# A sample turn's scores and values in six TensorE runs instead of twelve

## The chip, the core and the metric

The kernel runs on one core of a Trainium2 chip. The core has five engines that each work through their own list of instructions: PE (matrix products; PEld is its loading of weights), DVE (vectors), ACT (functions such as exp), POOL (a second vector engine) and SP, which here issues nearly all DMAs, one after the other. The metric is the device time of one execution in microseconds (us). A profile is one execution with a hardware trace. Names such as `out<-in,in` are the program's tiles, and L1290 is line 1290 of the kernel.

## What is computed

One step of a small decoder: a recurrent layer, then an attention layer with a forget gate. There are two inputs. The prompt is one new sequence of 2048 tokens. The sample is 8 sequences of 8 new tokens each, and each of them attends to 4096 earlier keys and values, which lie in a cache of pages of 128 rows and are found through a page table. The part that the change touches is the sample's attention, 16 heads of 64 numbers, all in 32-bit floats:

```python
s = jnp.einsum('bqhd,bkhd->bhqk', q, k).astype(jnp.float32) * (HEAD_DIM ** -0.5)
s = s + jnp.swapaxes(cq, 1, 2)[:, :, :, None] - jnp.swapaxes(ck, 1, 2)[:, :, None, :]
s = jnp.where(mask[None, None], s, -jnp.inf)
p = jax.nn.softmax(s, axis=-1)
return jnp.einsum('bhqk,bkhd->bqhd', p.astype(v.dtype), v)
```

## The kernel before, in words

The prompt's work fills PE from the first microsecond to the last: projections with every product split in three (tiles `kv`, `qg`, lines L387 to L389), then the prompt's attention (scores `st` in L1651 and L1652, row maxima `sx` in L1438, products with the values `ops` in L1675), then the output projection (`y`). The sample's attention is laid beside it.

**A turn** is one of the 8 sample sequences with one half of the heads; there are 16 turns. A turn reads 32 pages of keys and 32 of values, four pages to a tile of 1 MB (`raw`, L1144 and L1146, four DMAs on SP). So it has eight key tiles k0 to k7 and eight value tiles v0 to v7. A key tile is turned by two DVE transposes into `ktr` (L1218). After four key tiles (a group) the two halves pp = 0 and 1 of the heads can each be scored: 32 small matmuls `dS<-ktr,qw` of 32 by 128 (L1202; the trace shows 64 of them, two for each). They write one bank of PSUM, and DVE subtracts that from the tile `sc` (L1207) and takes a maximum (L1208) before the next scores may use the bank. `softmax` then does the maxima (`dm`), the exponentials on ACT, the sums (`dsum`) and transposes `sc` on DVE. A value tile is multiplied by eight small matmuls `dO<-raw,sc` of 32 by 256 (L1290; 16 in the trace), and the last one, v7, takes the new tokens' own rows in as well (`dO<-rawn,dpc`, L1295). The result goes out through `ob` and `dres`. Small matmuls of `dS` and `dO` use a quarter of the array's columns each, four such column groups side by side.

**A run** is a row of such small matmuls on PE with nothing between them: `together` (L124) issues the first matmul of a list, and binds the rest right behind it. With `beside=True` the first one may not come ahead of the prompt's latest score matmul (`place["T"]`, `behind`, L115). With `after` the first one waits for the DMAs that are given. Two runs can also happen to fall next to each other.

**The order.** The first two turns run beside the projections with `ahead=False`, each turn by itself. The other 14 run with `ahead=True`: `period` mixes the values of turn t with the keys of turn t+1, in the order v5 (of the turn before), k0, v6, k1, v7, k2, k3, v0, k4, v1, k5, v2, k6, v3, k7, v4. The tiles share four buffers (`nraw` = 4), so a tile is asked for when the tile that had its buffer has been transposed (keys) or multiplied (values). `Later` puts a run off by one or two ticks, and `Side` paces all of it beside the prompt's work by estimated costs. A scheduler then sets the final order on each engine from those instructions, their priorities and their dependencies.

Of the kernel before, what the change touches and what calls it, by code (L numbers as in the profile page):

```python
# [90 lines left out]
def tile_hawk_fox(  # L91
# [18 lines left out]
    def tt(eng, out, a, b, op):  # L110
        eng.tensor_tensor(out, a, b, op=op)  # L111
# [990 lines left out]
    def decode(es, turns, nraw, nktr, ahead):  # L1102
# [24 lines left out]
        def bank(name, tag="d"):  # L1127
            return psum["dec"].tile([P, 512], F32, name=name, tag=tag, bufs=1)
# [42 lines left out]
        class Turn:  # L1171


            def __init__(self, it):
                self.b, self.hg, self.odd = *turns[it], it % 2
                self.next = turns[it + 1] if it + 1 < len(turns) else None
                self.dl, self.raws = Later(), []

        def begin(t):
            t.gmx = pool.tile([P, 3, 8], F32, name="gmx", tag="gmx")  # L1180
            G.memset(t.gmx[:, 2, :], NEG)

        def keys(t, xs):
# [12 lines left out]
            def scores(g, pp, kt):  # L1196

                sp = bank("dS", "d" if ahead or pp == 0 else "o")

                def score(h, x, c):  # L1200
                    i0 = (h * 2 + x) * 32 + c * 8
                    return T.matmul(sp[c * 32:(c + 1) * 32, h * P:(h + 1) * P], qw[:, pp * 2 + h // 2, h % 2 * 2 + x, :],  # L1202
                                    kt[:, :, :, i0:i0 + 8], start=(x == 0), stop=(x == 1))

                together([partial(score, h, x, c) for h in range(4) for x in range(2) for c in range(4)], beside=True)
                sv = t.sc[:, g * 4:(g + 1) * 4, :, pp * 4:(pp + 1) * 4, :].rearrange("p n a h i -> p h (n a) i")
                tt(V, sv, sp[:, :].rearrange("p (h n i) -> p h n i", h=4, n=16), sv, ALU.subtract)  # L1207
                V.tensor_reduce(gmx[:, g, pp * 4:(pp + 1) * 4], sv, axis=AX.XY, op=ALU.max)  # L1208

            for x in xs:  # L1210
                g, n = divmod(x, 4)
                if n == 0:
                    t.kts = [pool.tile([P, 4, 4, 256], F32, name="ktr", tag="ktr", bufs=nktr) for _ in range(2)]
                raw, _ = pages(cache_k, b, hg, x)
                if x == (3 if ahead else 0):
                    fetch_c()
                for pp in range(2):
                    behind("V", V.transpose(t.kts[pp][:, n], raw[:, :, pp * 256:(pp + 1) * 256]).ins)  # L1218
# [58 lines left out]

        def values(t, xs):

            dl = t.dl  # L1280
            b, hg, pc = t.b, t.hg, t.pc
            if xs[0] == 0:
                t.op = bank("dO", "o")
            op = t.op

            def products(i, raw, came, rown=None):

                def mm(m, a):
                    c = ((i + m) % 2 * 2 + a) * 32
                    return T.matmul(op[c:c + 32, :256], t.sc[:, i // 4, m, a * 4:(a + 1) * 4, :].rearrange("p h q -> p (h q)"),  # L1290
                                    raw[:, m, a * 256:(a + 1) * 256],
                                    start=(i + m < 2), stop=(i + m == NPG - 1))
# [5 lines left out]
                mms = [partial(mm, m, a) for m in range(4) for a in range(2)]  # L1298
                if rown is not None:
                    mms += [partial(new, a) for a in range(2)]  # L1300
                together(mms, came, True)

            for x in xs:
                raw, came = t.raws.pop(0) if t.raws else pages(cache_v, b, hg, x)
                if x == 5:
                    t.rown = new_rows(b, hg)
# [3 lines left out]
                dl.tick()  # L1310
                yield 2 * PV
            if xs[-1] < 7:
                return
            dl.flush()
# [13 lines left out]
        def period(p, t, n):  # L1328


            chain_ = softmax(t)
            if n:
                begin(n)
            for who, x in (("v", 5), ("k", 0), ("v", 6), ("k", 1), ("v", 7), ("k", 2), ("k", 3), ("v", 0), ("k", 4),
                           ("v", 1), ("k", 5), ("v", 2), ("k", 6), ("v", 3), ("k", 7), ("v", 4)):
                if (who, x) == ("v", 0):
                    yield from chain_
                if who == "k" and n:
                    yield from keys(n, [x])
                elif who == "v" and (t if x < 5 else p):  # L1340
                    yield from values(t if x < 5 else p, [x])
                if x > 4 or who == "k" and x < 4:
                    yield from islice(chain_, 2)
# [6 lines left out]
        yield from keys(ts[0], range(8))  # L1350
        if ahead:
            for p, t, n in zip([None] + ts, ts, ts[1:] + [None]):
                yield from period(p, t, n)
            yield from values(ts[-1], [5, 6, 7])
        else:
            for t, n in zip(ts, ts[1:] + [None]):
# [658 lines left out]
```

## Time and profile before

| | us |
|---|---|
| median of 3 timed runs | 2931.59 |
| lowest, highest | 2919.55, 2937.87 |
| the profiled execution's own time | 2919.81 |
| its span in the trace | 2918.1 |
| its mean granted TensorE clock | 0.978 |

The profile's page gives the busy time of each engine and the span in 40 slices of 73 us. A timeline lists one engine's instructions in order of time: start, length, engine, line, operation, tiles, shape and count of equal ones that follow each other, and in brackets the idle time before it with what ended it. Matmuls overlap, so the room that one takes is read from start to start, not from its length. The list of waits says which instruction stood idle for which, how long in all, how often, and the longest.

### The profile page before, as it was taken

The page shows a single profiled execution, that of the slowest core. Times are in us where ns is not written, and L with a number is a line of the kernel's source. Part 1 is how long each engine was busy: PE and PEld are TensorE (multiplying, and loading weights), DVE is VectorE, ACT ScalarE, POOL GpSimd, SP SyncE. Part 2 cuts the span into 40 slices and gives each one's busy share as a digit, 9 for nine tenths or more (in the row PEclk, how much of TensorE's full clock was granted, in tenths as well). Part 3 has the DMA queues.
Part 4 walks back from the last instruction along what each step waited for, and adds up shares of the span by engine and source line. Part 5 has one row for each costly group of instructions (what it writes and reads, how often), then busy time and mean ns, then how long its engine had stood idle before and what let it go on. Part 6 is the DMA issues. An engine that isn't in the chain of part 4 may idle for free.

```text
span 2918.1 us, 59421 instructions
## 1 busy us (share of the span) xinstructions
PE 2747.1 (94%) x21086; PEld 2224.8 (76%) x21086; DVE 1828.1 (63%) x3971; ACT 1267.6 (43%) x2874; POOL 1098.0 (38%) x1207
## 2 busy tenths in 40 slices
PE   5998999999998999999999999999999999999998
PEld 5997789988898997887888766565666665666787
DVE  7877457244256775676565676767677766655465
ACT  4656342222234665533334345444444544455221
POOL 1654110000003652100001265756565655659554
PEclk9999999999999999999999999999999999999999
DMA  4224536789745536689999978778788777862454
GB/s 127 80 86 125 169 124 188 203 243 300 224 142 177 178 107 191 215 303 325 341 314 333 338 261 293 239 255 277 253 271 269 255 259 240 284 222 61 131 184 131
DMA packets 484789, 636.03 MB, mean 218 GB/s; under 512 B 100888, under 2 KB 293145, under 8 KB 477276
## 3 DMA queue, kind: packets, MB, share of 16 engines
q1 hardware_dynamic: 484204, 630.13, 66.6%
q8 instruction: 167, 2.74, 0.4%
q0 software_dynamic: 288, 2.10, 0.3%
q14 instruction: 130, 1.06, 0.1%
HBM read 512.78 MB, written 133.85 MB: 222 GB/s over the span
## 4 chain that ended last, share of the span: by engine, by line
PE 55%; DMA 9%; DVE 7%; ACT 4%; SPq 3%; issue 2%; POOL 1%; DVEq 0%; ACTq 0%; POOLq 0%
PE ops L1675 8%; PE st L1651 5%; PE sx L1438 4%; PE st L1652 4%; PE dS L1202 3%; PE dO L1290 3%; PE y L389 3%; PE y L387 3%; PE y L388 3%; DMA raw<-in_cache_k_dram 2%; PE kv L387 2%; PE kv L389 2%; PE kv L388 2%; PE qg L387 2%; PE qg L389 2%
## 5 line engine op out<-in xcount | busy, mean ns | idle before, releaser
L1218 DVE STREAM_TRANSPOSE ktr<-raw 128x1024 f32<-128x1024 f32 x256 | 308.0, 1225 | 97.6 <-DMA raw<-in_cache_k_dram 73.5
L1440 DVE TENSOR_REDUCE mxs<-sx 128x1 f32<-128x512 f32 x384 | 253.8, 680 | 157.6 <-PE sx L1438 156.8
L387 PE MATMUL kv<-wh,xh 128*128 128x256 f32 (+3 forms) x1088 | 307.7, 287 | 3.0 <-ACT wh L432 1.7
L389 PE MATMUL kv<-wh,xl 128*128 128x256 f32 (+3 forms) x1088 | 307.1, 284 | 0.4 <-DMA xl<-xld 0.4
L388 PE MATMUL kv<-wl,xh 128*128 128x256 f32 (+3 forms) x1088 | 306.6, 284 | 0.4 <-DVE wl L433 0.3
L433 DVE SCALAR_TENSOR_TENSOR wl<-wst,gv,wh 128x256 fp32r<-128x256 f32 (+1 forms) x384 | 171.1, 494 | 130.7 <-ACT wh L432 130.6
L432 ACT ACTIVATE wh<-wst,gv 128x256 fp32r<-128x256 f32 (+1 forms) x384 | 164.4, 499 | 200.4 <-DMA wst<-in_b_w_in_dram 83.0
L389 PE MATMUL qg<-xh,wl 128*128 128x384 f32 (+2 forms) x640 | 227.5, 357 | 2.2 <-DVE wl L433 2.2
L387 PE MATMUL qg<-xh,wh 128*128 128x512 f32 (+2 forms) x640 | 229.2, 359 | 0.0
L388 PE MATMUL qg<-xl,wh 128*128 128x512 f32 (+2 forms) x640 | 228.1, 358 | 0.0
L387 PEld LDWEIGHTS kv<-wh,xh 128*128 128x128 f32 (+1 forms) x1088 | 201.1, 186 | 8.7 <-issue 3.7
L389 PEld LDWEIGHTS kv<-wh,xl 128*128 128x128 f32 (+1 forms) x1088 | 202.3, 186 | 3.1 <-issue 2.4
L388 PEld LDWEIGHTS kv<-wl,xh 128*128 128x128 f32 (+1 forms) x1088 | 201.5, 186 | 4.1 <-issue 2.5
L1166 POOL TENSOR_TENSOR qw<-qb,amask 128x128 f32<-128x128 f32 x64 | 26.7, 422 | 459.9 <-PE dS L1202 197.7
L1662 ACT ACTIVATE attl<-st 128x512 f32<-128x512 f32 (+3 forms) x236 | 120.5, 524 | 129.2 <-PE st L1652 61.4
L1444 DVE CUSTOM_DVE_ANT_0 sx<-sx,maskb 128x128 f32<-128x128 f32 (+3 forms) x256 | 123.1, 488 | 70.9 <-PE sx L1438 64.9
L1662 ACT ACTIVATE attw<-st 128x512 f32<-128x512 f32 (+3 forms) x224 | 118.0, 550 | 102.4 <-PE st L1652 68.1
L1290 PE MATMUL dO<-raw,sc 128*32 128x256 f32 x2048 | 141.9, 398 | 20.7 <-DMA raw<-in_cache_v_dram 19.9
L111 POOL TENSOR_TENSOR atth<-atth,attl 128x512 f32<-128x512 f32 (+3 forms) x119 | 128.1, 1079 | 65.9 <-ACT attl L1662 47.7
L111 POOL TENSOR_TENSOR atth<-atth,attw 128x512 f32<-128x512 f32 (+3 forms) x116 | 132.3, 1141 | 38.9 <-ACT attw L1662 22.1
L1202 PE MATMUL dS<-ktr,qw 128*32 128x128 f32 x4096 | 129.8, 282 | 14.4 <-DVE ktr L1218 13.5
L925 ACT COPY kf<-kv 128x256 f32<-128x256 f32 (+1 forms) x136 | 49.0, 366 | 217.1 <-PE kv L389 152.7
(359 smaller groups left out, 7651.8 us busy)
## 6 DMA issues: line engine op xcount, KB each, us to landing
raw<-in_cache_k_dram SPq DMA_DIRECT2D x512, 256.0 KB
raw<-in_cache_v_dram SPq DMA_DIRECT2D x512, 256.0 KB
wst<-in_w_kv_dram SPq DMA_DIRECT2D x48, 512.0 KB
wst<-in_b_w_in_dram SPq DMA_DIRECT2D x48, 512.0 KB
xt<-in_x_prompt_dram SPq DMA_DIRECT2D x32, 512.0 KB
wst<-in_a_w_in_dram SPq DMA_DIRECT2D x64, 256.0 KB
out_dram<-kf SPq DMA_DIRECT2D x128, 128.0 KB
cb<-cd SPq DMA_DIRECT2D x14, 1024.0 KB
```

The source lines that it names most:

```text
L111: eng.tensor_tensor(out, a, b, op=op)
L387: T.matmul(ps, lh(k), rh(k), start=(k == 0), stop=False)
L388: T.matmul(ps, lh(k), rl(k), start=False, stop=False)
L389: end = T.matmul(ps, ll(k), rh(k), start=False, stop=(k == nk - 1))
L432: A.activation(wh[:, k, :], st[:, k, :], AF.Copy, scale=gk)
L433: V.scalar_tensor_tensor(wl[:, k, :], st[:, k, :], gk, f(wh[:, k, :]), op0=ALU.mult, op1=ALU.subtract)
L1202: return T.matmul(sp[c * 32:(c + 1) * 32, h * P:(h + 1) * P], qw[:, pp * 2 + h // 2, h % 2 * 2 + x, :], kt[:, :, :, i0:i0 + 8], start=(x = ...
L1218: behind("V", V.transpose(t.kts[pp][:, n], raw[:, :, pp * 256:(pp + 1) * 256]).ins)
L1290: return T.matmul(op[c:c + 32, :256], t.sc[:, i // 4, m, a * 4:(a + 1) * 4, :].rearrange("p h q -> p (h q)"), raw[:, m, a * 256:(a + 1) * ...
L1440: r = V.reduce_max(mx[:, j, ck:ck + 1], ps[:, :w], axis=AX.X)
L1662: pair.append((k, lo, p, A.activation(p[:, lo:], ps[:, lo:], AF.Exp)))
L1675: return T.matmul(ops[r * HD:(r + 1) * HD, a0 * P:], vvs[h % 2][:, k, :], p[:, :].rearrange("p (a r c) -> p a r c", a=2, r=2)[:, a0:, r, : ...
```

## The change

The twelve runs of a turn (four of scores, eight of values) become six. `beside` issues one run from the matmuls of one scores call (if there is one) and of one or two value tiles. `both` puts the scores of pp = 0 and one value tile in one run, and the scores of pp = 1 and the next value tile in another; it is called for v0 and v1 with the first key group of the next turn, and for v4 and v5 with the second. `pair` puts two value tiles in one run: v2 with v3, v6 with v7. The order of a period becomes k0, k1, v6 and v7 (of the turn before), k2, k3, both (v0, v1), k4, k5, pair (v2, v3), k6, k7, both (v4, v5). In `ahead` mode nothing is put off through `Later` any more. The new tokens' rows become four matmuls of 128 columns on all four column groups, ahead of the others of v7, instead of two of 256 columns on two groups at the end. The two turns without `ahead` get only this last edit.

```diff
             def __init__(self, it):
                 self.b, self.hg, self.odd = *turns[it], it % 2
                 self.next = turns[it + 1] if it + 1 < len(turns) else None
-                self.dl, self.raws = Later(), []
+                self.dl, self.raws, self.kts = Later(), [], {}
...
+        def scores(t, g, pp):
+
+            kt, sp = t.kts[g][pp], bank("dS", "d" if ahead or pp == 0 else "o")
...
+            def taken():
+                sv = t.sc[:, g * 4:(g + 1) * 4, :, pp * 4:(pp + 1) * 4, :].rearrange("p n a h i -> p h (n a) i")
+                tt(V, sv, sp[:, :].rearrange("p (h n i) -> p h n i", h=4, n=16), sv, ALU.subtract)
+                V.tensor_reduce(t.gmx[:, g, pp * 4:(pp + 1) * 4], sv, axis=AX.XY, op=ALU.max)
+
+            return [partial(score, h, x, c) for h in range(4) for x in range(2) for c in range(4)], taken
+
+        def fetch_v(t, x):
+
+            raw, came = t.raws.pop(0) if t.raws else pages(cache_v, t.b, t.hg, x)
+            if x == 5:
+                t.rown = new_rows(t.b, t.hg)
+            return t, x, raw, came
+
+        def products(t, x, raw, came):
+
+            if x == 0:
+                t.op = bank("dO", "o")
+            op, i = t.op, x * 4
...
+            def new(e, a):
+                c, half = (e * 2 + a) * 32, slice(e * P, (e + 1) * P)
+                return T.matmul(op[c:c + 32, half], t.pc[:, a * 32:(a + 1) * 32],
+                                t.rown[:, a * 256:(a + 1) * 256][:, half], start=False, stop=False)
+
+            return ([partial(new, e, a) for e in range(2) for a in range(2) if x == 7]
+                    + [partial(mm, m, a) for m in range(4) for a in range(2)])
+
+        def beside(n, g, pp, *vs):
+
+            mms, taken = scores(n, g, pp) if n else ([], None)
+            together(mms + [mm for v in vs for mm in products(*v)], [d for v in vs for d in v[3]], True)
+            if taken:
+                taken()
...
-                    if n == 3:
-                        dl.after(1 + pp, lambda g=g, pp=pp, kt=t.kts[pp]: scores(g, pp, kt))
+                    if n == 3 and not ahead:
+                        dl.after(1 + pp, lambda g=g, pp=pp: beside(t, g, pp))
...
-                def new(a):
-                    return T.matmul(op[a * 32:(a + 1) * 32, :256], pc[:, a * 32:(a + 1) * 32],
-                                    rown[:, a * 256:(a + 1) * 256], start=False, stop=True)
...
-                dl.after(2 if ahead and x == 0 else 1,
-                         lambda i=x * 4, raw=raw, came=came, rown=t.rown if x == 7 else None: products(i, raw, came, rown))
...
+        def pair(t, x):
+
+            vs = [fetch_v(t, x)]
+            yield 4 * PV
+            vs.append(fetch_v(t, x + 1))
+            yield 2 * PV
+            beside(None, 0, 0, *vs)
+            yield 2 * PV
+            if x == 6:
+                yield from result(t)
+
+        def both(n, g, t, x):
+
+            if t and not n:
+                yield from pair(t, x)
                 return
...
+            for pp in range(2):
+                vs = [fetch_v(t, x + pp)] if t else []
+                yield 2 * PV * len(vs)
+                beside(n, g, pp, *vs)
+                yield 2 * PV * len(vs)
...
-            for who, x in (("v", 5), ("k", 0), ("v", 6), ("k", 1), ("v", 7), ("k", 2), ("k", 3), ("v", 0), ("k", 4),
-                           ("v", 1), ("k", 5), ("v", 2), ("k", 6), ("v", 3), ("k", 7), ("v", 4)):
-                if (who, x) == ("v", 0):
-                    yield from chain_
...
+            for x in range(4):
+                if x == 2 and p:
+                    yield from pair(p, 6)
+                    yield from islice(chain_, 2)
+                if n:
+                    yield from keys(n, [x])
+                yield from islice(chain_, 2)
+            yield from chain_
+            yield from both(n, 0, t, 0)
+            for x in range(4, 8):
+                if x == 6:
+                    yield from pair(t, 2)
+                if n:
+                    yield from keys(n, [x])
+            yield from both(n, 1, t, 4)
```

On PE, in the middle of the prompt's attention, a scores run and a value run of the kernel before stand like this, with the prompt's `mps`, `st` and `sx` between them:

```order
L1202 MATMUL dS<-ktr,qw 32x128 x32
L1457 MATMUL mps<-ident,st_s 128x128
L1651 MATMUL st<-qa_17882,atth 128x512
L1652 MATMUL st<-qbt_17880,atth 128x512
L1438 MATMUL sx<-atth,attl 128x128
L1438 MATMUL sx<-atth,attl 128x256
L1651 MATMUL st<-qa_17882,atth 128x512
L1652 MATMUL st<-qbt_17880,atth 128x512
L1290 MATMUL dO<-raw,sc 32x256 x8
```

In the changed kernel PE has, about there (the scores are L1189 now, the values L1214):

```order
L1694 MATMUL st<-qa_17888,atth 128x512
L1695 MATMUL st<-qbt_17886,atth 128x512
L1189 MATMUL dS<-ktr,qw 32x128 x32
L1214 MATMUL dO<-raw,sc 32x256 x8
L1481 MATMUL sx<-atth,qbt_17884 128x128
L1481 MATMUL sx<-atth,qbt_17884 128x512
```

The value tile's eight matmuls have moved up right behind the scores. The end of a turn's values stands on PE before the change as a run by itself, v7 and the new rows:

```order
L1654 MATMUL st<-attw 128x128
L1290 MATMUL dO<-raw,sc 32x256 x8
L1295 MATMUL dO<-rawn,dpc_13980 32x256 x2
L1457 MATMUL mps<-ident,st_s 128x128
L1438 MATMUL sx<-kbt_17878,qbt_17879 128x512 x2
```

and after the change as v6, the new rows and v7 in one:

```order
L1695 MATMUL st<-qbt_17884,atth 128x512
L1214 MATMUL dO<-raw,sc 32x256 x8
L1220 MATMUL dO<-rawn,dpc_13984 32x128 x4
L1214 MATMUL dO<-raw,sc 32x256 x8
L1500 MATMUL mps<-ident,st_s 128x128
```

The new rows have gone from two matmuls of 256 columns behind v7 to four of 128 between v6 and v7.

## Rows read from the trace of the kernel before

**Rows 1.** The profile's page: PE's busy time, and DMA share in 40 slices (tenths).

```profile
PE 2747.1 (94%) x21086; PEld 2224.8 (76%) x21086; DVE 1828.1 (63%) x3971; ACT 1267.6 (43%) x2874; POOL 1098.0 (38%) x1207
...
DMA  4224536789745536689999978778788777862454
```

**Rows 2.** Tile `dO`, 1340 to 2600 us: min/median/max ns, first and last start.

```profile
L1290 PE MATMUL dO<-raw,sc x1792: 376/379/637, 1348.2 to 2595.2; 128*32 128x256 f32 x200
```

**Rows 3.** Stretches: length, busy time by engine, granted clock, DMA share, GB/s.

```profile
1345.00:1640.00 295.00, 287.83 (x2690) 246.95 (x2689) 171.84 (x342) 108.98 (x277) 17.56 (x30) 0.99 0.99 332
...
2000.00:2400.00 400.00, 379.04 (x3482) 245.78 (x3484) 281.23 (x579) 192.45 (x487) 242.74 (x237) 0.97 0.78 260
```

**Rows 4.** PE's waits, 1345 to 2600 us: total us, times, longest.

```profile
PE dO L1290 <- DMA raw<-in_cache_v_dram: 13.5, 6, 3.4
PE sx L1438 <- DVE mxs L1440: 7.1, 11, 1.5
```

**Rows 5.** Timeline of PE: one value tile as a run by itself.

```profile
2531.97 0.40 PE L1651 MATMUL st<-qa,ka 128*128 128x512 f32 x1
2532.21 0.39 PE L1652 MATMUL st<-attl,kbt 128*128 128x512 f32 x1
2532.53 1.07 PE L1290 MATMUL dO<-raw,sc 128*32 128x256 f32 x16
2533.53 0.50 PE L1651 MATMUL st<-qa,ka 128*128 128x512 f32 x1
2533.87 0.40 PE L1652 MATMUL st<-attl,kbt 128*128 128x512 f32 x1
```

**Rows 6.** Timeline of PE: two value tiles that fell next to each other.

```profile
2409.81 0.40 PE L1652 MATMUL st<-qbt,atth 128*128 128x512 f32 x1
2410.14 1.93 PE L1290 MATMUL dO<-raw,sc 128*32 128x256 f32 x32
2412.01 0.50 PE L1651 MATMUL st<-qa,atth 128*128 128x512 f32 x1
2412.34 0.39 PE L1652 MATMUL st<-qbt,atth 128*128 128x512 f32 x1
```

**Rows 7.** Timeline of PE: a scores run by itself.

```profile
2497.49 0.39 PE L1652 MATMUL st<-qbt,kbt 128*128 128x512 f32 x1
2497.81 1.95 PE L1202 MATMUL dS<-ktr,qw 128*32 128x128 f32 x64
2499.69 0.50 PE L1651 MATMUL st<-attl,ka 128*128 128x512 f32 x1
2500.03 0.40 PE L1652 MATMUL st<-qbt,kbt 128*128 128x512 f32 x1
```

**Rows 8.** Timeline of PE: scores and one value tile that fell next to each other.

```profile
1629.32 0.39 PE L387 MATMUL qg<-xh,wh 128*128 128x512 f32 x1
1629.63 1.95 PE L1202 MATMUL dS<-ktr,qw 128*32 128x128 f32 x64
1631.41 1.05 PE L1290 MATMUL dO<-raw,sc 128*32 128x256 f32 x16
1632.38 0.51 PE L388 MATMUL qg<-xl,wh 128*128 128x512 f32 x1
1632.73 0.39 PE L389 MATMUL qg<-xh,wl 128*128 128x512 f32 x1
```

**Rows 9.** Timeline of PE: v7 with the new rows, and what follows.

```profile
2289.22 1.07 PE L1290 MATMUL dO<-raw,sc 128*32 128x256 f32 x16
2290.11 0.60 PE L1295 MATMUL dO<-rawn,dpc 128*32 128x256 f32 x4
2290.64 0.50 PE L1438 MATMUL sx<-atth,qbt 96*128 96x512 f32 x1
```

**Rows 10.** Timeline of SP: the issue of one value tile.

```profile
2230.28 3.14 SPq L1146 DMA_DIRECT2D raw<-in_cache_v_dram  x4
```

**Rows 11.** Timeline of PE: the run that waited for that tile.

```profile
2238.59 1.07 PE L1290 MATMUL dO<-raw,sc 128*32 128x256 f32 x16 [3.35 <-DMA raw<-in_cache_v_dram]
```

More of the change, by code (lines that the diff above doesn't have):

```diff
@@ L1181, in begin, with score, mm @@
             G.memset(t.gmx[:, 2, :], NEG)
+        def scores(t, g, pp):
+            kt, sp = t.kts[g][pp], bank("dS", "d" if ahead or pp == 0 else "o")
+            def score(h, x, c):
+                i0 = (h * 2 + x) * 32 + c * 8
+                return T.matmul(sp[c * 32:(c + 1) * 32, h * P:(h + 1) * P], qw[:, pp * 2 + h // 2, h % 2 * 2 + x, :],
+                                kt[:, :, :, i0:i0 + 8], start=(x == 0), stop=(x == 1))
+            def taken():
[12 more added lines that the diff above has]
+            op, i = t.op, x * 4
+            def mm(m, a):
+                c = ((i + m) % 2 * 2 + a) * 32
+                return T.matmul(op[c:c + 32, :256], t.sc[:, x, m, a * 4:(a + 1) * 4, :].rearrange("p h q -> p (h q)"),
+                                raw[:, m, a * 256:(a + 1) * 256],
+                                start=(i + m < 2), stop=(i + m >= NPG - 2))
+            def new(e, a):
[9 more added lines that the diff above has]
+                taken()
         def keys(t, xs):
@@ L1194, in fetch_c @@
                 S.dma_start(t.cn[:, :, :], sn_d[hg, sl, :, sl])
[L1196 to L1208, printed above, removed]
             for x in xs:
@@ L1212, in keys @@
                 if n == 0:
-                    t.kts = [pool.tile([P, 4, 4, 256], F32, name="ktr", tag="ktr", bufs=nktr) for _ in range(2)]
+                    t.kts[g] = [pool.tile([P, 4, 4, 256], F32, name="ktr", tag="ktr", bufs=nktr) for _ in range(2)]
                 raw, _ = pages(cache_k, b, hg, x)
@@ L1217, in keys @@
                 for pp in range(2):
-                    behind("V", V.transpose(t.kts[pp][:, n], raw[:, :, pp * 256:(pp + 1) * 256]).ins)
-                    if n == 3:
-                        dl.after(1 + pp, lambda g=g, pp=pp, kt=t.kts[pp]: scores(g, pp, kt))
+                    behind("V", V.transpose(t.kts[g][pp][:, n], raw[:, :, pp * 256:(pp + 1) * 256]).ins)
+                    if n == 3 and not ahead:
+                        dl.after(1 + pp, lambda g=g, pp=pp: beside(t, g, pp))
                     if (g, n, pp) == (1, 0, 0):
@@ L1278, in values @@
         def values(t, xs):
[L1280 to L1292, printed above, removed]
-                def new(a):
-                    return T.matmul(op[a * 32:(a + 1) * 32, :256], pc[:, a * 32:(a + 1) * 32],
-                                    rown[:, a * 256:(a + 1) * 256], start=False, stop=True)
[L1298 to L1301, printed above, removed]
@@ L1303, in values @@
-            for x in xs:
-                raw, came = t.raws.pop(0) if t.raws else pages(cache_v, b, hg, x)
-                if x == 5:
-                    t.rown = new_rows(b, hg)
-                dl.after(2 if ahead and x == 0 else 1,
-                         lambda i=x * 4, raw=raw, came=came, rown=t.rown if x == 7 else None: products(i, raw, came, rown))
+            for x in xs:
+                v = fetch_v(t, x)
+                t.dl.after(1, lambda v=v: beside(None, 0, 0, v))
                 yield 2 * PV
-                dl.tick()
+                t.dl.tick()
@@ L1311, in values @@
                 yield 2 * PV
-            if xs[-1] < 7:
-                return
-            dl.flush()
+            t.dl.flush()
+            yield from result(t)
[7 more added lines that the diff above has]
+            if x == 6:
+                yield from result(t)
+        def both(n, g, t, x):
+            if t and not n:
+                yield from pair(t, x)
+                return
+            for pp in range(2):
[3 more added lines that the diff above has]
+                yield 2 * PV * len(vs)
@@ L1315, in values, with result @@
+        def result(t):
+            b, hg, op = t.b, t.hg, t.op
             ob = pool.tile([P, 256], F32, name="ob", tag="ob")
@@ L1333, in period @@
                 begin(n)
-            for who, x in (("v", 5), ("k", 0), ("v", 6), ("k", 1), ("v", 7), ("k", 2), ("k", 3), ("v", 0), ("k", 4),
-                           ("v", 1), ("k", 5), ("v", 2), ("k", 6), ("v", 3), ("k", 7), ("v", 4)):
-                if (who, x) == ("v", 0):
-                    yield from chain_
-                if who == "k" and n:
-                    yield from keys(n, [x])
[L1340 to L1343, printed above, removed]
+            for x in range(4):
[3 more added lines that the diff above has]
+                if n:
+                    yield from keys(n, [x])
+                yield from islice(chain_, 2)
[7 more added lines that the diff above has]
+            yield from both(n, 1, t, 4)
         fetch_q(turns[0][0])
@@ L1349, in decode @@
         begin(ts[0])
-        yield from keys(ts[0], range(8))
         if ahead:
+            for g in range(2):
+                yield from keys(ts[0], range(g * 4, g * 4 + 4))
+                yield from both(ts[0], g, None, 0)
             for p, t, n in zip([None] + ts, ts, ts[1:] + [None]):
                 yield from period(p, t, n)
-            yield from values(ts[-1], [5, 6, 7])
+            yield from pair(ts[-1], 6)
         else:
+            yield from keys(ts[0], range(8))
             for t, n in zip(ts, ts[1:] + [None]):
```

## The prediction, made before the changed kernel ran

> **What bounds the kernel now.** I read the page first: PE is busy for 94% of the span and no other engine for more than 63% (PEld is a part of PE's own work) [rows 1]. Then the stretches, to see whether that holds where the sample's turns lie, which is from 1348 us (the first value run of the 14 mixed turns) to 2595 us [rows 2]. It does: 287.8 of 295 us in the last of the projections and 379.0 of 400 us in the attention [rows 3]. So PE's own list sets the time, and an instruction that takes less room there brings the end forward, as long as nothing that PE waits for comes in its place. Two things could. The DMA engines are full in the first of these stretches, share 0.99 at 332 GB/s, while in the attention the share is 0.78 [rows 3]; the 40 slices show the same as a block of nines and then sevens and eights [rows 1]. And PE already waits for value pages, 13.5 us in 6 waits, the longest 3.4 us; the next cause, sx for DVE's maxima, makes 7.1 us [rows 4].
>
> Last I read the small matmuls in PE's timeline, from start to start, since their lengths overlap. Ordinary 512-column matmuls follow at 0.24 us (2531.97 to 2532.21) [rows 5]. A run costs more than its matmuls at both borders: the step into it is 0.32 us, and the first ordinary matmul after it keeps its successor off for 0.34 us [rows 5]. Where two runs fell next to each other these borders are paid once [rows 6, 8]. That gives the price that the change is about.
>
> **The runs that go.** I take each run from the start of the last ordinary matmul before it to the start of the second one after it, less two ordinary steps of 0.24 us. One value tile: 2533.87 - 2532.21 - 0.48 = 1.18 us [rows 5]. Two in one: 2412.34 - 2409.81 - 0.48 = 2.05 us [rows 6], so joining two saves 2 x 1.18 - 2.05 = 0.31 us. Scores: 2500.03 - 2497.49 - 0.48 = 2.06 us [rows 7]. Scores with one value tile: 1632.73 - 1629.32 - 0.48 = 2.93 us [rows 8], so joining these saves 2.06 + 1.18 - 2.93 = 0.31 us as well. Counted in PE's order, the 14 mixed turns had 151 runs (17 of the 168 had fallen together by chance) and have 85 after the change, of which four are the first turn's scores, with no values beside them. 66 runs go: 66 x 0.31 = **20.5 us** off PE.
>
> **The new rows.** From v7's first matmul to the next ordinary one is 1.42 us with them [rows 9] and 1.00 us without [rows 5], so the two matmuls cost 0.42 us. They stand on two of four column groups while the other two are idle; four matmuls of half the width on all four groups carry half as much on each. No row shows that form. It can save 0 (if the four cost as before) to 0.42 us (if they vanish between v6 and v7); I take half, 0.21 us, since a group's work halves. 16 turns: **3.4 us** (0 to 6.7). Together 24 us less on PE.
>
> **What is moved.** No DMA, transpose, subtraction or exponential is added or dropped; their order changes. The tiles were asked for in turns of keys and values, and now come as k, k, v, v, so that keys hand their buffers to keys and values to values. A value tile may be asked for when the run of the tile two before it has ended. Between a `pair` and the next `both` stand two key tiles and a part of softmax, so the lead is a third of a turn less the run: about 89 us (2595 - 1348 = 1247 us for 14 turns) / 3, or 10 to 20 us by place, where a tile took 8.3 us from its issue to its use when the use was waiting for it (2230.28 to 2238.59) [rows 10, 11]. So I expect the present waits for value pages to shrink. Bounds: all 13.5 us go, or none [rows 4]; I take half, **6.8 us**. On SP's queue the issue of a value tile waits for a run on PE, and the prompt's loads stand behind it; that is so now as well, and neither of PE's two longest kinds of wait is for those loads [rows 4], so I cost it at nothing.
>
> One new wait I do charge. The second tile of a `pair` can be asked for only after the run of scores and v1 has ended. At the closest place in PE's new order there are 28 ordinary matmuls between that run and the pair, 15 of them 512 wide, at 0.24 us at most 6.7 us, against 8.3 us needed. I charge **+3 us** (0 to the longest wait seen, 3.4 us); elsewhere more than that lies between.
>
> The joined run waits at its head for the keys' transposes, the value page and, inside, for softmax; the page used to hold back the values alone. Behind it on PE stands everything. DVE's subtraction waits for the last score only, so it starts where it did; the next scores need the bank that it frees, and between them now lie the value tile's 0.9 us and some ordinary matmuls, against 0.7 us for the subtraction. I cost this at nothing; the cover is the lead of the pages, and without it the price is in rival D.
>
> **Where the DMAs are full.** The first stretch holds 295 / 89 = 3.3 of the 14 turns, that is 24 x 3.3 / 14 = 5.7 us of the saving. With the DMA engines' share at 0.99 the pages cannot come sooner [rows 3], so I take this as given back: **+5.7 us** (0 to 5.7). The Trainium skill ("DMA: Bandwidth & Descriptors", Specifications) gives HBM's limit for one core as about 358 GB/s. By that page the stretch's 332 GB/s has 7% left, the 5.7 us would stay saved, and the time would be 2904 us; no row here shows the chip at that limit, so I keep the share of 0.99.
>
> **The sum.** -20.5 - 3.4 - 6.8 + 3 + 5.7 = -22 us. The profiled execution took 2919.8 us, so it would be 2898 us. The median of the three timed runs is 2931.6 us, 0.4% above it, and carries the same -22: **2910 us**.
>
> **The rivals.**
> *A, the forecast (chance 0.5):* as summed, 2900 to 2919 us.
> *B, the waits go altogether (0.2):* the even spacing k, k, v, v removes all of the 13.5 us and the full DMAs give nothing back: 2931.6 - 24 - 13.5 = 2894 us. For it: the leads above exceed 8.3 us nearly everywhere. Against: the 0.99.
> *C, the room on PE turns into waits (0.2):* PE still has to get its exponentials from ACT and its maxima from DVE, and a longer block of sample work hands them a burst behind it. The waits for DVE's maxima, 7.1 us now [rows 4], and others grow by what PE gains: 2925 to 2932 us. For it: PE's idle share in the attention is already 5% [rows 3]. Against: no other engine is above 70% there (DVE, 281.2 of 400) [rows 3].
> *D, slower (0.1):* the head of a double run waits for its second page. Place: the 30 double value runs. Price: the mean of the present waits, 13.5 / 6 = 2.25 us [rows 4], 67.5 us in all, less the 13.5 that go and the 24 saved: 2931.6 + 30 = 2962 us. It decides from (24 + 13.5) / 30 = 1.25 us per double run on. For it: at the closest place the lead is shorter than 8.3 us. Against: that is one place of 14. The Trainium skill ("TensorE: Matmul & The Clock Gate", Part 3, on row and column tiling) says that matmuls start and end strictly in program order, so that a waiting head would hold back the prompt too. By that rule the whole wait is lost; the trace agrees, PE stood idle for 3.35 us with prompt matmuls behind [rows 11].
> That the change does not do what it says is left without a chance: PE's order shows the six runs of each turn.
>
> **How the numbers follow.** 1% of 2931.6 is 29 us, about what a measurement of this kernel can tell from no change: faster means below 2902, slower above 2961. B is faster, and the fast edge of A (0.08); D is slower; the rest is the same: 0.28, 0.62, 0.10. The range leaves out D and the outer edges of B and C, and takes in the 0.3% by which timed runs differ: 2888 to 2933 us. A alone is 2900 to 2919.
>
> **What would show it.** Right: 85 runs in PE's timeline from the third turn on; scores with values at 2.9 us and double tiles at 2.05 us by the measure above; v6, new rows and v7 about 0.2 us longer than a double tile; waits of PE for value pages at 4 to 10 us in all; the last value run some 15 to 25 us earlier. Wrong: idle time before double runs in the list of waits, with a value page as its end (D); a total of PE's waits for DVE and ACT that has grown by 15 us or more (C); a first stretch that has not become shorter would confirm the charge for full DMAs, one shorter by 5 us refute it.

## The result: 0.4% slower, and the profile after

The changed kernel takes 2935.2 us (median of 16 runs, 2925.2 to 2944.3), the kernel before 2923.1 us in 16 runs next to them (2911.6 to 2937.9): 1.0044 times as long, 95% interval 1.0029 to 1.0058. That is within 1%, but it is 12 us slower where 22 us of gain were forecast, and it is above the range. (The three runs that the forecast started from, 2931.6 us, lay 8 us above the median of the 16; without that the miss would be 34 us, not 25.) The profiled execution of the change took 2937.8 us (span 2936.1), that of before 2919.8.

What answers to [rows 1, 3], from the page and the list of stretches (length, busy time by engine, granted clock, DMA share, GB/s):

```profile
PE 2741.1 (93%) x21150; PEld 2237.0 (76%) x21150; DVE 1831.4 (62%) x3971; ACT 1268.6 (43%) x2874; POOL 1101.6 (38%) x1207
...
1345.00:1640.00 295.00, 280.17 (x2661) 244.23 (x2662) 169.43 (x336) 104.80 (x267) 16.69 (x28) 0.98 0.99 328
2000.00:2400.00 400.00, 371.11 (x3491) 244.42 (x3484) 277.42 (x574) 187.17 (x474) 236.73 (x232) 0.95 0.79 261
```

PE is busy 6 us less, but its gaps have grown: 371 of 400 us in the attention where it was 379. In the same 400 us it issued 3491 matmuls against 3482, hardly more. The mean granted clock there fell from 0.97 to 0.95: PE spent more of the stretch at the lower of its two levels (1.2 and 2.4 GHz).

What answers to [rows 8], [rows 6] and [rows 9], PE's timeline: scores with a value tile; a double run; v6, the new rows, v7.

```profile
2125.19 0.40 PE L1695 MATMUL st<-attl,kbt 128*128 128x512 f32 x1
2125.52 1.96 PE L1189 MATMUL dS<-ktr,qw 128*32 128x128 f32 x64
2127.29 1.05 PE L1214 MATMUL dO<-raw,sc 128*32 128x256 f32 x16
2128.26 0.50 PE L1694 MATMUL st<-qa,ka 128*128 128x512 f32 x1
2128.60 0.39 PE L1695 MATMUL st<-attl,kbt 128*128 128x512 f32 x1
...
2241.94 1.93 PE L1214 MATMUL dO<-raw,sc 128*32 128x256 f32 x32 [0.20 <-issue]
2243.81 0.50 PE L1694 MATMUL st<-attl,ka 128*128 128x512 f32 x1
...
2109.86 1.07 PE L1214 MATMUL dO<-raw,sc 128*32 128x256 f32 x16
2110.75 0.40 PE L1220 MATMUL dO<-rawn,dpc 128*32 128x128 f32 x8
2110.97 1.05 PE L1214 MATMUL dO<-raw,sc 128*32 128x256 f32 x16
```

The room is as forecast: 2128.60 - 2125.19 - 0.48 = 2.93 us for scores with values, the double run 1.87 us to its successor as before, the new rows 0.22 us where they took 0.42.

What answers to [rows 4], PE's waits from 1345 to 2600 us (total us, times, longest), first in the change, then two rows of before that stand beside the `sx` row of [rows 4]:

```profile
PE mps L1500 <- DVE st_s L1496: 20.9, 9, 5.9
...
PE sx L1481 <- DVE mxs L1487: 18.1, 14, 4.9
...
PE sx L1481 <- DVE mxs L1483: 10.1, 10, 3.9
...
PE dO L1214 <- DMA raw<-in_cache_v_dram: 2.6, 1, 2.6
```

```profile
PE sx L1438 <- DVE mxs L1444: 5.8, 5, 2.3
...
PE mps L1457 <- DVE st_s L1453: 2.5, 2, 2.2
```

DVE's two longest kinds of wait for loads in the attention, 1640 to 2600 us, in the change and then before. The first is for key pages; the second is for a small load, the sums of the prompt's softmax:

```profile
DVE ktr L1254 <- DMA raw<-in_cache_k_dram: 25.5, 11, 6.4
DVE atth L1557 <- DMA atth<-atth: 12.0, 2, 8.1
```

```profile
DVE ktr L1218 <- DMA raw<-in_cache_k_dram: 9.7, 4, 5.1
...
DVE atth L1514 <- DMA atth<-atth: 1.9, 2, 1.2
```

PE's waits for value pages went from 13.5 us to 2.6. In their place PE waits for DVE's row maxima, 49 us by these three rows, 15 before (the kinds are the same: a bank of `sx` that DVE has not read, and `st_s`, the finished maxima). And DVE, on whose maxima the attention hangs, waits there 25.5 us for key pages instead of 9.7, and 12.0 for the sums instead of 1.9. One place shows how a late load of DVE makes PE wait. SP's queue, then DVE, then PE:

```profile
2228.02 3.19 SPq L1146 DMA_DIRECT2D raw<-in_cache_v_dram  x4
...
2233.12 3.03 SPq L1146 DMA_DIRECT2D raw<-in_cache_v_dram  x4
...
2239.01 0.71 SPq L1552 DMA_DIRECT2D atth<-atth  x1
```

```profile
2245.97 0.35 DVE L1557 RECIPROCAL atth<-atth 128x32 f32<-128x32 f32 x1 [8.11 <-DMA atth<-atth]
...
2248.05 3.49 DVE L1254 STREAM_TRANSPOSE ktr<-raw 128x1024 f32<-128x1024 f32 x3
2251.47 0.67 DVE L1487 CUSTOM_DVE_ANT_0 sx<-sx,maskb 128x512 f32<-128x512 f32 x1
...
2252.22 0.17 DVE L1496 TENSOR_REDUCE st_s<-mxs 128x4 f32<-128x16 f32 x1
```

```profile
2246.35 0.23 PE L1697 MATMUL st<-attw 128*128 128x128 bf16 x1
2252.44 0.48 PE L1500 MATMUL mps<-ident,st_s 128*128 128x128 f32 x1 [5.86 <-DVE st_s L1496]
```

The pages of two value tiles are asked for ahead of the sums, and DVE goes on 7 us after the sums' own ask. DVE stands 8.1 us at that load; then come three transposes of keys, and the row maxima last. PE waits 5.9 us for them. At 2173.5 us a key page does the same: DVE idle 6.4 us, PE 4.5. The waits for the sums alone do not set the change apart, though: kernels 4 to 6 below, which lose no time against the kernel before, wait 11 to 12 us for them too.

PE's clock fell at that place. The stretches ahead of the wait's end, around it and behind it:

```profile
2240.00:2250.00 10.00, 6.10 (x48) 3.28 (x47) 3.96 (x6) 4.30 (x8) 8.99 (x8) 1.00 0.48 181
2251.00:2257.00 6.00, 4.56 (x19) 2.57 (x21) 2.64 (x6) 1.11 (x4) 0.35 (x1) 0.50 0.76 237
2258.00:2268.00 10.00, 10.00 (x60) 6.65 (x56) 8.25 (x15) 5.30 (x11) 4.83 (x6) 1.00 0.95 311
```

PE stood idle from 2246.6 to 2252.4 us, and from 2251 to 2257 the granted clock was 0.50, its lower level: two `sx` matmuls of 512 columns right behind the wait took 1.20 us, and 0.71 us at 2260.65.

### The profile page after: what moved, and what is told of

The parts are those of the page before. It is cut to its first block, busy times and chain, and to the rows that moved or that the text cites. A ratio compares the mean times of both kernels' runs of the same rounds, so it can differ in the third digit from the quotient of the medians.

```text
span 2936.1 us, 59533 instructions
## 1 busy us (share of the span) xinstructions
PE 2741.1 (93%) x21150; PEld 2237.0 (76%) x21150; DVE 1831.4 (62%) x3971; ACT 1268.6 (43%) x2874; POOL 1101.6 (38%) x1207
## 3 DMA queue, kind: packets, MB, share of 16 engines
q1 hardware_dynamic: 484204, 630.13, 66.1%
## 4 chain that ended last, share of the span: by engine, by line
PE 60%; DVE 12%; DMA 12%; ACT 6%; SPq 4%; issue 3%; POOL 1%; DVEq 0%; ACTq 0%; POOLq 0%
PE ops L1718 8%; PE y L389 4%; PE y L388 4%; PE y L387 4%; PE st L1694 4%; DMA raw<-in_cache_k_dram 4%; PE sx L1481 4%; PE dS L1189 3%; PE st L1695 3%; PE dO L1214 3%; PE qg L387 3%; PE kv L389 3%; PE kv L387 3%; PE qg L389 3%; PE qg L388 3%
## 5 line engine op out<-in xcount | busy, mean ns | idle before, releaser
L1705 ACT ACTIVATE attw<-st 128x512 f32<-128x512 f32 (+3 forms) x224 | 118.5, 549 | 116.6 <-PE st L1695 66.7
L1214 PE MATMUL dO<-raw,sc 128*32 128x256 f32 x2048 | 135.8, 386 | 9.6 <-DMA raw<-in_cache_v_dram 8.4
L111 POOL TENSOR_TENSOR atth<-atth,attw 128x512 f32<-128x512 f32 (+3 forms) x116 | 132.3, 1141 | 32.2 <-ACT attw L1705 19.2
L1189 PE MATMUL dS<-ktr,qw 128*32 128x128 f32 x4096 | 130.8, 283 | 12.5 <-DVE ktr L1254 11.7
```

The costliest lines, as they stand in the source:

```text
L1214: return T.matmul(op[c:c + 32, :256], t.sc[:, x, m, a * 4:(a + 1) * 4, :].rearrange("p h q -> p (h q)"), raw[:, m, a * 256:(a + 1) * 256], ...
L1705: pair.append((k, lo, p, A.activation(p[:, lo:], ps[:, lo:], AF.Exp)))
```

## The experiments

The recorded expectations call PE TensorE and DVE VectorE. A tile's lead is the time from its first ask on SP to its first use.

Two theories at the start. **Late loads:** the joins save their room; but double value runs need two value tiles at once, so tiles come as k, k, v, v, key pages reach DVE with less to spare, and its late maxima cost PE more than the joins save. **Long runs:** the joined runs themselves delay the prompt's maxima. A third reading, tied to neither, is a chance of placing.

For each kernel the table has its time over that of the kernel before in the same comparison, and from its profile, 1340 to 2600 us (leads 1640 to 2600): separate sample runs on PE after 1345 us, the idle time summed over PE's instructions, the part of it that DVE ended, and the median leads.

| kernel | us | ratio (95%) | runs | PE idle | for DVE | lead of keys | of values |
|---|---|---|---|---|---|---|---|
| before | 2923.1 | 1 | 147 | 59.1 | 25.2 | 19.2 | 12.2 |
| before, second profile | 2918.6 | 0.9996 (0.9983-1.0010) | 147 | 56.0 | 26.0 | 19.1 | 12.5 |
| change | 2935.2 | 1.0044 (1.0029-1.0058) | 81 | 79.8 | 57.4 | 13.5 | 16.5 |
| 1 all runs apart | 2924.3 | 1.0001 (0.9981-1.0020) | 118 | 78.9 | 49.6 | 15.7 | 15.1 |
| 2 pairs apart | 2929.8 | 1.0010 (0.9988-1.0032) | 85 | 75.1 | 57.5 | 13.4 | 16.2 |
| 3 scores and value apart | 2929.7 | 1.0024 (1.0005-1.0042) | 112 | 77.6 | 45.1 | | |
| 4 tiles in turn, scores joined | 2897.8 | 0.9912 (0.9894-0.9929) | 112 | 55.7 | 32.1 | 16.0 | 16.7 |
| 5 tiles in turn, all apart | 2925.1 | 1.0006 (0.9986-1.0025) | 149 | 66.1 | 32.7 | 18.6 | 14.5 |
| 6 as 4, maximum of cn later in the program | 2894.1 | 0.9906 (0.9879-0.9934) | 112 | 58.0 | 33.4 | 16.1 | 16.2 |
| 7 as 6, v6 and v7 paired | 2917.2 | 0.9985 (0.9969-1.0000) | 97 | 71.0 | 45.6 | 14.7 | 16.3 |
| 8 before, identity for keys | 2969.0 | 1.0165 (1.0147-1.0182) | 140 | 89.2 | 68.9 | | |
| 9 change, identity for keys | 2942.1 | 1.0076 (1.0060-1.0092) | 80 | 86.9 | 62.3 | | |
| 10 before, one page a key tile | 2909.8 | 0.9959 (0.9943-0.9974) | 147 | 56.7 | 24.1 | | |
| 11 change, one page a key tile | 2892.3 | 0.9897 (0.9877-0.9918) | 82 | 56.6 | 33.5 | | |

**Can single profiles carry this?** The kernel before once more, no edit.

> The kernel before once more, word for word, for a second profile: how far two profiles of one kernel differ in TensorE's idle time and in its waits for VectorE from 1340 to 2600 (59.1 and 25.2 us in the first). If single profiles can carry the comparison, within 8 us of those; if they can't, the 25 to 57 us of the change may be a chance of the profiled execution. Time: 2918 to 2930 us.

Idle 56.0 us and 26.0 for DVE: within 3 us of the first. The 80 and 57 of the change are not a chance of one execution.

**1, all runs apart.** In `beside`:

```
-            together(mms + [mm for v in vs for mm in products(*v)], [d for v in vs for d in v[3]], True)
+            if mms:
+                together(mms, beside=True)
+            for v in vs:
+                together(products(*v), v[3], True)
```

> The changed kernel with its runs taken apart again (scores alone, each value tile alone, twelve runs a turn) and everything else kept: the tile order k, k, v, v, the places where pages are asked for, the new rows' columns. Theory 1 (late key pages: the joins do save their room, about 24 us by the medians of room, and the tile order loses more than that, because key pages then reach VectorE late, the row maxima behind them come late and TensorE waits): the waits stay and the room is lost, so it is slower than the changed kernel, 2945 to 2965 us against 2935, and TensorE's waits on st_s and on the banks of sx from 1340 to 2620 stay over 35 us (49 with the change, 15 before). Theory 2 (the long runs themselves pile up TensorE's maxima work and so make the waits): with runs as short as before the waits fall to about 15 us and the time to 2915 to 2928. Theory 3 (a chance of placing, tied to neither): no more than 5 us from the changed kernel, waits anywhere.

2924 us. The first theory's time missed by 20, the second's waits missed: `st_s` and the banks of `sx` still make 41 us by its list of waits, and idle time stays at 79. The first theory's reckoning was at fault: in this order separate runs stand side by side on PE anyway, 118 blocks and not 151, with 27 blocks of two value tiles where the change has 30, and the profiled execution (2932.3) was above the median. And 12 us less than the change, with 11 us of room given up, is not what it said. The run left both theories alive.

**8 and 9, nobody waits for a key page.** The same edit in both kernels, here in the changed one:

```
-V.transpose(t.kts[g][pp][:, n], raw[:, :, pp * 256:(pp + 1) * 256])
+V.transpose(t.kts[g][pp][:, n].rearrange("p m (a c) -> p (m a) c", c=P), ident[:, :].unsqueeze(1).to_broadcast([P, 8, P]))
```

> The kernel before, with VectorE's key transposes in the sample turns reading the identity tile in place of the key pages (same shape and count; the key pages are still fetched, and nobody waits for them, so the scores are meaningless). Both theories: VectorE's waits for key pages (9.7 us from 1640 to 2600) go, value pages come somewhat earlier; 2903 to 2918 us. It is the base for the same edit on the changed kernel.

> The changed kernel with the same edit: key transposes read the identity tile, key pages are fetched and nobody waits for them. Theory 1 (late key pages): the 25.5 us that VectorE waited for key pages from 1640 to 2600 go, TensorE's waits on st_s and on the banks of sx fall from 49 us to 20 or less, and it ends 15 to 25 us below the kernel before with that edit (2885 to 2898 us), as the room of the joins promised. Theory 2 (long runs make the waits): those waits stay at 40 us or more and it stays about 10 us above the kernel before with that edit. Theory 3: no more than 5 us apart.

The change ended 27 us below its base, a little more than the first theory said, yet both became slower, which nobody had expected. The waits from 1345 to 2600 us of the first, then of the second:

```profile
DVE gmx L1222 <- DMA cn<-snd: 54.6, 9, 12.3
PE sx L1438 <- DVE mxs L1440: 43.2, 16, 12.2
```

```profile
PE mps L1500 <- DVE st_s L1496: 43.8, 12, 9.2
DVE gmx L1258 <- DMA cn<-snd: 35.6, 8, 7.7
```

DVE no longer stood at key pages and so came too early to the next load behind them on SP, `cn` (the new tokens' scores): in kernel 8, by the median of the last 13 turns, it came there 1.1 us ahead of the load's ask, where before it came 5.9 us behind. PE's waits for maxima grew with it. So it need not be a key page: here another late load in DVE's order went with waits of PE. But the pair did not remove what it was meant to remove, and its 27 us prove nothing about the key pages.

**4, tiles in turn.** Key and value tiles alternate, the scores keep their value tile, four value tiles have runs of their own again:

```
             for x in range(4):
-                if x == 2 and p:
-                    yield from pair(p, 6)
-                    yield from islice(chain_, 2)
                 if n:
                     yield from keys(n, [x])
-                yield from islice(chain_, 2)
+                yield from islice(chain_, 2 if x else 4)
+                if p and x < 2:
+                    yield from one(p, 6 + x)
...
             for x in range(4, 8):
-                if x == 6:
-                    yield from pair(t, 2)
                 if n:
                     yield from keys(n, [x])
...
+                if x < 6:
+                    yield from one(t, x - 2)
```

> The changed kernel with eight runs a turn: each run of scores still goes on with a value tile, but the other four value tiles have runs of their own again, one behind each of k0, k1, k4 and k5, so that key and value tiles are asked for in turn where the change asks for two and two. Theory 1 (late key pages): the lead of key tiles from ask to use goes back from a median of 13.6 us towards 19, VectorE's waits for key pages from 25.5 us to 15 or less, and about 40 of the 66 joins are kept (13 us) with the new rows' 3: 2903 to 2922 us. Theory 2 (long runs make the waits): the runs of scores with a value tile stay, and with them over half of the extra waits: 2925 to 2940 us.

2898 us, faster than both kernels and by 5 us better than the first theory's range. Idle time is back at 56 us, and the lead of keys at 16.0 of the 19 hoped for. DVE's wait for key pages in the attention, 25.5 us in the change, fell to the 15 us that the first theory named:

```profile
DVE ktr L1254 <- DMA raw<-in_cache_k_dram: 15.1, 7, 4.3
```

**2, 3 and 5: which join, and which order.** The edits in short, not word for word:

```
 2:          if mms: together(mms + [...values...], ...)   else, per value tile: together(products(*v), v[3], True)
 3:          together(mms, beside=True); together([...values...], ..., True)
 5:          kernel 4 with the edit of experiment 1
```

> The changed kernel (2935 us) with only its double value runs taken apart into two runs each, placed where the double run was; scores still go on with a value tile and the tile order stays k, k, v, v. All runs apart gave 2924. If the double runs carry the cost of joining (they hold two buffers until both tiles are there, and 2.5 us of TensorE in one piece), this goes to 2915 to 2925; if the runs of scores with a value tile carry it, it stays at 2930 to 2940; if only the order k, k, v, v costs (the first theory as first stated), it goes up by the room of the joins undone, some 22 of 0.31 us: 2938 to 2945.

> The changed kernel with only the runs of scores and value taken apart (scores alone, then the value tile), double value runs kept, order kept. If the runs of scores with a value tile carry the cost of joining, 2912 to 2925 us; if the double value runs do, 2930 to 2940; if only the order costs, 2942 to 2950 (some 44 joins of 0.31 us undone).

> The kernel with key and value tiles in turn that ran in 2898 us, with its runs of scores and value taken apart as well, so that no run is joined in the program (where two stand next to each other on TensorE they still save the room between them) and only the order of the tiles and the new rows' columns differ from the kernel before. If the order k, v, k, v is what gained and the joins do save their room, 2903 to 2915 us; if joined runs cost more in waits than they save in room, as the 2924 of the changed kernel's runs apart against 2935 suggests, 2880 to 2896; if the gain was the joins' alone, 2918 to 2925.

The program of kernel 2 has the eight runs a turn of kernel 4 and differs in the order of tiles (and of two steps of `softmax`): 1.0010 / 0.9912, so k, k, v, v takes 1.0% longer, 29 us. Kernel 2 says little of the double runs by themselves, though: on PE 26 blocks of two value tiles are left of 30, for the two come one behind the other anyway (85 blocks, 81 in the change). (Such a run lasts 1.9 us, not 2.5.) So this 29 us is the price of the order together with the double runs that it brings.

In k, k, v, v joins do not pay. By the ratios, taking the double runs apart in the program gains 10 us (2), scores and values 6 us (3), both 12 us (1); the first two are about what the intervals allow. With tiles in turn the join of scores and value gains 0.9% (5 to 4, 27 us), more than its room, (149 - 112) x 0.31 = 11.5 us; PE's idle time falls with it, by 10 us in these profiles. With all runs apart the order makes no difference that can be measured (1 against 5): k, k, v, v has 13 us more idle time there, but lets 31 more runs fall together, 9.6 us. Kernel 5 thus came out where the gain would be "the joins' alone"; but in k, k, v, v the same join gains nothing (1 to 2). It takes both. DVE's waits for key pages in the attention go with the order, 25.0 and 26.1 us in 1 and 2, 10.3 and 15.1 in 5 and 4.

**10 and 11, fewer pages to load.** A key tile asks for one page and DVE transposes it four times over:

```
-            for i in range(4):
+            for i in range(1 if ahead and cache is cache_k else 4):
```

> The kernel before, in whose fourteen mixed turns a key tile loads one page in place of four and VectorE transposes it four times over (same transposes, same runs on TensorE, half the keys' and so five eighths of all the pages' bytes; the sample scores then hold one page four times). With the identity tile in place of the key pages, the loads behind them (cn) became the late ones, since the pages' asks still stood ahead of them on SP; here the asks themselves are fewer. Every theory: faster than the kernel before, by the time in which DMA is full (1345 to 1640) and by the page waits of both engines: 2890 to 2910 us. It is the base for the same edit on the changed kernel.

> The changed kernel with the same edit, one page to a key tile. If late loads in VectorE's strict order are what the tile order k, k, v, v costs, VectorE's waits for loads from 1340 to 2600 (80 us in the changed kernel, 44 before) come within 10 us of the base's, TensorE's waits for VectorE (57 against 25) likewise, and the joins show their room: 15 to 25 us below the base. If the long runs make TensorE wait by themselves, waits for VectorE stay 20 us or more above the base's and the time at or above the base.

The deciding pair. (One page of four is a quarter of the keys' bytes, not half; the five eighths of all bytes are right.) The change is now faster than its base, 0.9897 / 0.9959 = 0.994, 17.5 us by the medians, inside the 15 to 25 expected. PE's idle time is equal (56.6 and 56.7) and its waits for DVE 9 us apart, where the unedited kernels differ by 21 and 32; DVE's own waits for loads are 66 us against 64 in the base. PE's waits for maxima in the change with this edit, 1345 to 2600 us:

```profile
PE mps L1500 <- DVE st_s L1496: 13.3, 10, 3.0
...
PE sx L1481 <- DVE mxs L1487: 10.3, 14, 2.2
...
PE sx L1481 <- DVE mxs L1483: 7.0, 9, 2.4
```

They are 31 us where the change has 49, and the longest, 5.9 and 4.9 us, are 3.0 and 2.2. The long runs are all still there (82), and the kernel keeps the room that they save. They may not be wholly free: the base waits 16 us for maxima, but 14 us for value pages, which the change does not (2.5). The waits of DVE in the attention, 1640 to 2600 us, where the change has 12.0 and 25.5:

```profile
DVE atth L1557 <- DMA atth<-atth: 8.2, 3, 4.0
DVE ktr L1254 <- DMA raw<-in_cache_k_dram: 7.4, 3, 3.6
```

The base has no wait for a key page there. (Both have more of them ahead of 1640 us, 33 us and 52 in the base, where PE runs projections and no row maximum is needed.) The edit takes bytes and asks out of the way of every load, not of the keys' alone, so what it shows is late loads. That key pages count most among them is argued from DVE's waits in the change, 25.5 of 41.5 us for loads in the attention.

**6 and 7, a maximum put later, and a pair where leads are long.** The edits in short:

```
 6: -                    if (g, n, pp) == (1, 0, 0):
    +                    if (g, n, pp) == (1, 2, 0):
 7: the first half of a turn as in the change (k0, k1, pair of v6 and v7, k2, k3), else as 6
```

> The kernel with key and value tiles in turn (2898 us), with VectorE's maximum over the tile cn placed at the seventh key tile in place of the fifth. There VectorE waited for cn's load 3.2 us near 1919 us in that kernel, and TensorE 3.65 us behind it; with key pages that nobody waited for, those waits were 60 us and more. If late loads of whatever tile, in VectorE's strict order, are what costs, this saves the 3 to 5 us of that wait: 2890 to 2896 us; if such a wait is hidden, 2896 to 2900.

> The kernel with key and value tiles in turn and the maximum of cn at the seventh key tile (2894 us), with value tiles 6 and 7 in a double run again and k0, k1 ahead of them, as the change has it; tiles 2 and 3 keep runs of their own between k4, k5 and k6. If a pair costs only where key tiles stand close (the second half of a turn; tiles 6 and 7 have leads of over 20 us in the changed kernel), its join saves some 12 times 0.31 us: 2888 to 2893. If any double run costs, 2897 to 2910.

6 ran in 2894 us, 0.9% below the kernel before and inside the range expected, but that was luck, for its edit changed the program and not the order on DVE. In the traces of 4 and 6 DVE has the maximum at the same place among the key transposes in every turn, and still waits there for `cn`; the place near 1919 us in 4, then in 6:

```profile
1918.83 0.21 DVE L1258 TENSOR_REDUCE gmx<-cn 8x8 f32<-8x64 f32 x1 [3.16 <-DMA cn<-snd]
```

```profile
1909.79 0.21 DVE L1258 TENSOR_REDUCE gmx<-cn 8x8 f32<-8x64 f32 x1 [3.65 <-DMA cn<-snd]
```

So 6 is kernel 4 once more, and says nothing on the wait for `cn`; the order of 4 is the fastest of those that leave no work out. Its stretch of attention in 6, against 379 of 400 us at 0.97 [rows 3]:

```profile
2000.00:2400.00 400.00, 385.38 (x3728) 253.73 (x3728) 291.86 (x595) 198.72 (x501) 255.26 (x247) 0.99 0.84 280
```

7 missed: one pair a turn, at the place where pages had the longest leads, gives up 23 us, not a gain of 3. Its profile shows the same chain: the lead of k1 falls from 19.3 to 12.9 us (median), DVE waits for key pages 20 us in the attention (14 in 6) and for `cn` 17.3 us in 6 waits (5.4 in 6). PE's waits for value pages are 2.4 us in all, so it is not a long wait for the pair's own pages that costs. Whether it is the two key tiles side by side or the double run, 7 does not separate; and why a single pair costs 23 of the 41 us between kernel 6 and the change stays open.

## Why the prediction was wrong

**The runs that go: right.** 81 runs after 1345 us, and the four of the first turn lie ahead of that: the 85 counted; 2.93 us each for scores with values. **The new rows: right,** 0.22 us for 0.21. **Waits for value pages: mis-sized:** all six went, 13.5 us, where half was taken; the lead of the value tiles came out at 16.5 us, in the range given. **The new wait in a double run, +3: right in size by luck.** One head of 30 waited, 2.6 us, at the last v6 and v7 of all and not at the place that was named. So rival D fell.

**What is moved: this is the step that failed.** It said that "keys hand their buffers to keys and values to values", worked out the lead of a value tile, and left that of a key tile out. In the kernel before, values hand theirs to keys at many places, and value pages had the short leads (12 us against 19 for keys). The change evened that out the wrong way round: keys 13.5, values 16.5. PE lost 11 us of waits for values, and DVE got 16 us more for keys and 10 for the sums in the attention; PE's waits for DVE's maxima rose from 15 to 49 us. That the loads behind the page asks cost "nothing" rested on [rows 4], on PE's own waits: the table showed what ended PE's waits one step back, DVE, and not what DVE waited for. And the cover that the prediction named for the joined run, the lead of the pages, went for the keys.

**Full DMAs: right in sign, the reason not shown.** From the last `tps` matmul, ahead of all changed work, to the last `kv` matmul is 376.9 us in the change, 373.8 and 370.5 in the two profiles before, so the first stretch did not get shorter. Its share stayed at 0.99, at 328 GB/s. But PE's idle time in it went from 7 and 5 us to 15, with the projections' own operands as the longest waits, and no run separates the DMA engines' share from that.

**Rival C** named the sign that came, waits for DVE and ACT grown by 15 us or more (72 us against 43 by the sums of idle time), and ended at 2932. The reason that it gave, the burst of maxima after long runs, is at most a part: experiment 11 has the long runs with 31 us of those waits, not 49, and keeps the gain.

**The sum as it came out,** from the start of the last `tps` matmul to the end, which leaves out what the executions differ by ahead of the changed work: 1699.6 us in the change, 1686.7 and 1684.5 before, 14 us more. Room 66 x 0.31 = -20.5; new rows -3; idle time 88.3 against 66.7 and 66.6, +22; mean granted clock 0.968 against 0.975 and 0.977, by (0.976 - 0.968) x 1700 at most +14, and +9 if what falls into the idle time is left out. Together +7 to +12 against 14 measured. So the new waits ate the room, and the clock made the change slower. The clock is a term that the prediction lacks. That the longer waits brought it down is shown at the place above and argued for the rest; over all timed runs its mean is 0.979 before, 0.972 with the change, and 0.980 in kernel 6. For kernel 6 the same sum gives -25 (room -10.9, new rows -3, idle time -3, clock -8.5) against -26 measured. It does not close everywhere: for kernel 11 it is 8 us too low.

## What to carry to other kernels

Before moving loads about, list for every engine what its own waits are for, not only for the engine that bounds: an engine at 63% whose order mixes loads with work that the bound engine needs at once is the path by which a late load gets there. If tiles of two kinds share buffers, work out the lead of each kind, for a new order gives one what it takes from the other. Joining small runs paid here (27 us) where key and value tiles alternated, and not where they came two by two. And before a result is read as a test of an edit, see in the trace that the edit changed the order on the engine: that of kernel 6 did not, and that of kernel 2 hardly.

## What the runs showed of the hardware that was not expected

Taking a wait away can cost more than the wait: with DVE's key pages made free (8), it stood 54.6 us at the next load of the same queue, and the kernel lost 1.65%. And a wait of PE can cost more than its length: behind one of 5.86 us the granted clock was 0.50 from 2251 to 2257 us, with 1.00 ahead of it and behind. Over the part of the span behind the last `tps` matmul, 22 us more idle time went with a mean granted clock lower by 0.008, worth up to 14 us.
